# Memory products of block 2's second layer moved into block 1's norms, first layer's memory kept in DRAM, two modulations on VectorE

## The chip, the cores and the metric

The kernel runs on one core of a Trainium2 chip. The metric is the device time of one execution in microseconds, the median of the runs. PE is the matrix engine (TensorE), DVE VectorE, ACT ScalarE, POOL GpSimd; SP's queue issues the transfers.

## The reference

Two blocks work on a sequence of 256 tokens with 1024 channels in float32. Block 1 has two layers. In each, six modulation vectors are made from a condition vector, and each of two norms is scaled and shifted by a pair of them:

```python
mod = c_act @ w_ada[l] + b_ada[l]
sh1, sc1, g1, sh2, sc2, g2 = [t[:, None, :] for t in jnp.split(mod, N_ADA, axis=-1)]
h = rmsnorm(x, norm_mix_g[l]) * (1.0 + sc1) + sh1
z = h @ w_in[l]
...
x = x + g1 * (o @ w_out[l])
h = rmsnorm(x, norm_mlp_g[l]) * (1.0 + sc2) + sh2
x = x + g2 * (jnp.square(jax.nn.relu(h @ w_up[l])) @ w_down[l])
```

(o comes from four attention mixers on slices of z.) A last rmsnorm gives the input of block 2. Each of block 2's two layers has three branches: a state-space scan in two directions (32 heads), a differential attention of 8 heads, and a cross attention to a fixed memory of 256 tokens. The gated branches are summed, go through an output product, and end in a layer norm:

```python
mem_kv = jnp.einsum('bmd,de->bme', mem, w_mem_kv[layer]).reshape(
    Bsz, MEM_TOKENS, 2, CROSS_HEADS, CROSS_HEAD_DIM)
oc = _memory_cross_attention(cq.reshape(Bsz, S, CROSS_HEADS, CROSS_HEAD_DIM), mem_kv)
...
out = jnp.einsum('bsd,de->bse', merged, w_out[layer])

x = _layernorm(DEEPNORM_ALPHA * x.astype(jnp.float32) + out,
               ln_g[layer], ln_b[layer]).astype(x.dtype)
```

`mem_kv` holds the memory's keys and values. They depend on nothing that the blocks compute, so their products can stand anywhere before the layer that uses them.

## The kernel before

**Products.** Activations lie with channels on the partitions. Every product is split for accuracy: a weight tile `w` [128x1024] is cast to `wh` on ACT (L300) and the rest `wl` is taken on DVE (L302); the activations have a high and a low part too, and three products (h·wh, l·wh, h·wl, all at L328) are accumulated. A key piece of the memory is 48 products of 256 columns, a value half 48 products of 512 columns (`mem_gemm`, six pieces a layer: four for the keys, two for the values).

**Weights.** `stream` lists the weight tiles in the order of use, `next_w` takes the next one and at that time issues the transfers of the first eight entries of the list (L290, SP's queue) and splits the first four. There are eight buffers for `w` and four each for `wh` and `wl`.

**Order.** The program is written as one stream of instructions for all engines; a scheduler orders each engine's list at build time by readiness and priority. Fillers are closures in a queue: `fill` emits the next ones, `need` all up to a tag. Each engine then runs its list in order.

**Units.** Large activations live in eleven buffers of [128x2048] (`unit`). Whoever asks for a unit when all are taken waits in the schedule until the oldest user is done. In block 2 such units are, among others, `xh`, `xl` (the layer's input), `dq`, `dk`, `dv` (differential attention), `ysh`, `ysl` (the scan's output, two each), `mk` and `mv` (the memory).

**Norms.** `rms_wide` squares x on ACT, folds the squares on DVE, sums over partitions on PE (`st`), takes the rest on DVE (`rv`) and POOL (`rsy`, a power of -1/2, L394), and spreads it with PE (`bc`). Then DVE and ACT make `ah` and `al` (L590 to L592), slice by slice, and the next products start. In block 1 PE does a modulation (`ada`, 64 rows in the trace) meanwhile: the one for (layer 0, vector 5) in the norm before the first MLP, (1,2) and (1,3) before layer 1's mixers, (1,4) before the second MLP. In the first MLP POOL makes (1,0) and (1,1) with multiplications of its own (`sb`, L570 and L572), in the second (1,5). Before the final norm lies the second half of the first layer's memory values.

**Layer norm between block 2's layers.** The mean and the variance need two such rounds: st, mu, bc, subtraction (L1662), squares, folds, st, rv, rsy, bc. All six memory products of the second layer (`mem_gemm`, tile names mh and ml) are emitted there, and the scheduler spreads them over the rounds.

**Heads.** `diff` makes one head of the differential attention: scores (`ds`), softmax on DVE and ACT (`sm`, `E`), turning (`tw`), values (`do`); after four heads a norm on POOL scales their outputs (`rsy`, then eight times `dq`, L1603), and eight transposes (`dtp`, L1607) turn them. Fillers are emitted between the heads.

Of the kernel before, what the change touches and what calls it, by code (L numbers as in the profile page):

```python
# [216 lines left out]
AHEAD_W, AHEAD_S = 8, 4  # L217
# [8 lines left out]
class Emit:  # L226
# [100 lines left out]
    def mm(self, o, l, r, start, stop):  # L327
        self.nc.tensor.matmul(o, l, r, start=start, stop=stop)  # L328
# [37 lines left out]
    def tok_mm(self, ps, t, act, k, w, j, st, sp):  # L366

        wh, wl = (x[:, j * 512 : (j + 1) * 512] for x in w)
# [116 lines left out]
def block1(e, ctx, mem0):  # L485
# [3 lines left out]
    mhl, mk0, mv0 = mem0  # L489
# [16 lines left out]
    start = [[], a0[0:2], a0[2:4], a0[4:6], a0[6:8]]  # L506
    for k in range(MEM):
        e.stream(MEM_KEYS(0)[k], *start[k])
    for l in range(DEPTH):
        W = lambda i: ("w_in1", l, zorder[i])  # L510
        ea, am = ad_early(l), ad_mix(l)
        e.stream(*([] if l else [W(0)]), W(1), W(2), *ea[0:2], ("cmp_k1", l), W(3), *ea[2:3], ("cmp_v1", l), W(4), *ea[3:4], W(5))
        e.stream(W(6), *am[0:2], ("w_out1", l, 0), *am[2:3], W(7), ("w_out1", l, 1), *am[3:4], W(8), *am[4:])
        e.stream(("w_out1", l, 2), ("w_out1", l, 3), ("w_up", l, 0), *ad_norm(l))
# [6 lines left out]
        e.stream(("w_down", l, 15), *([("w_in1", l + 1, zorder[0])] if l + 1 < DEPTH else []), *ad_next(l))  # L521
    e.stream(*MEM_KEYS(0)[MEM:])
# [13 lines left out]
    boxes = {}  # L536
# [36 lines left out]

    def ada_rows(l, s):
# [8 lines left out]
    def norm_stats(src):  # L583
        return e.rms_wide(ap_, src, 1e-6)
# [23 lines left out]
    e.need("start4")  # L608

# [98 lines left out]
    def mixers(l, ah, al, oh, ol, ev_x):  # L708
# [258 lines left out]
        e.need("I")  # L967
        e.need("ad")
# [4 lines left out]
    for l in range(DEPTH):  # L973
# [4 lines left out]
        if l:  # L978
            bc0 = norm_stats(x)
            e.need("next")  # L980
# [12 lines left out]
        ada_add("norm", ad_norm(l))  # L993
        bc0 = norm_stats(x)
# [7 lines left out]
        def ev_up(g):  # L1002
            def ev(ps):
# [4 lines left out]
                last["act"] = nc.scalar.activation(uh, r, AF.Square)  # L1008
                nc.vector.tensor_tensor(r, r, ps, ALU.mult)
                last["dve"] = nc.vector.tensor_tensor(ul, r, uh.bitcast(F32), ALU.subtract)  # L1010
# [34 lines left out]
        def late_mem():  # L1045
            with tc.issue_after(last["dve"].ins), tc.issue_after(last["act"].ins):
                box.append(load_mem(e))

        parts, box, last = {}, [], {}
        steps = mlp_keys(l)  # L1050
        for g in range(17):
            if l + 1 == DEPTH and g == 1:
                e.add("mlp", late_mem)
# [7 lines left out]
            ada_add("mlp", steps.get(g, []))  # L1061
            for i, p in enumerate(ad_mlp(l)):
# [3 lines left out]
        ada_add("next", ad_next(l))  # L1066
# [14 lines left out]
    return xh, xl  # L1081
# [3 lines left out]
def block2(e, ctx, xh, xl, mk, mv, out):  # L1085
# [68 lines left out]
    for l in range(DEPTH):  # L1154
# [17 lines left out]
        if l + 1 < DEPTH:  # L1172
            e.stream(*MEM_KEYS(l + 1))
# [534 lines left out]
```

## Time and profile before

| | us |
|---|---|
| median of 3 runs (1836.12 to 1838.73) | 1838.46 |
| the profiled execution | 1837.75 |
| its span | 1835.9 |
| PE busy | 1785.1 (97% of the span) |
| DVE busy | 1332.7 (73%) |
| ACT busy | 1017.0 (55%) |
| POOL busy | 360.6 (20%) |

A busy PE is not a PE at its peak: products are pipelined, and the granted clock can be at either of two levels. The page gives the granted clock as a share of 2.4 GHz, so 0.50 is 1.2 GHz. Where PE has nothing to wait for, products of 256 columns follow each other every 0.12 us although each row shows 0.28. In the timelines, a row's bracket names the idle time of that engine before the row and what ended it; "x64" joins 64 like instructions in one row.

### The profile page before, as it was taken

The page shows a single profiled execution, that of the slowest core. Times are in us where ns is not written, and L with a number is a line of the kernel's source. Part 1 is how long each engine was busy: PE and PEld are TensorE (multiplying, and loading weights), DVE is VectorE, ACT ScalarE, POOL GpSimd, SP SyncE. Part 2 cuts the span into 40 slices and gives each one's busy share as a digit, 9 for nine tenths or more (in the row PEclk, how much of TensorE's full clock was granted, in tenths as well). Part 3 has the DMA queues.
Part 4 walks back from the last instruction along what each step waited for, and adds up shares of the span by engine and source line. Part 5 has one row for each costly group of instructions (what it writes and reads, how often), then busy time and mean ns, then how long its engine had stood idle before and what let it go on. Part 6 is the DMA issues. An engine that isn't in the chain of part 4 may idle for free.

```text
span 1835.9 us, 36208 instructions
## 1 busy us (share of the span) xinstructions
PE 1785.1 (97%) x14320; PEld 1671.4 (91%) x14320; DVE 1332.7 (73%) x2204; ACT 1017.0 (55%) x1882; POOL 360.6 (20%) x291
## 2 busy tenths in 40 slices
PE   7999899999998999999999999999999999999997
PEld 6778799987878999998999999999998999999996
DVE  3566775756768655798897997566788797997565
ACT  4444444444554444567777575454556777575452
POOL 0000282800007300002444202200001444202200
PEclk9999999999998999999999999999999999999999
DMA  8874876768347655553444644465554445644451
GB/s 330 305 233 159 316 259 199 254 201 294 128 143 280 225 181 184 170 170 122 159 162 152 195 159 145 167 206 174 196 175 138 150 154 158 194 162 162 151 183 57
DMA packets 98219, 346.82 MB, mean 189 GB/s; under 512 B 12288, under 2 KB 13440, under 8 KB 97792
## 3 DMA queue, kind: packets, MB, share of 16 engines
q1 hardware_dynamic: 98048, 344.50, 55.7%
q8 instruction: 112, 1.84, 0.4%
q14 instruction: 59, 0.48, 0.1%
HBM read 339.01 MB, written 1.05 MB: 185 GB/s over the span
## 4 chain that ended last, share of the span: by engine, by line
PE 91%; DVE 3%; ACT 3%; DMA 2%; issue 1%; POOL 0%; SPq 0%; POOLq 0%; DVEq 0%; ACTq 0%
PE g L328 68%; PE acc L328 10%; PE yps L328 2%; PE ada L328 1%; PE o L328 1%; DVE wl L302 1%; PE sc L328 1%; PE ds L328 1%; ACT wh L300 1%; PE do L328 1%; PE xs L328 1%; PE xo L328 1%; ACT sb L666 1%; DMA w<-w_up 1%; PE tp L691 1%
## 5 line engine op out<-in xcount | busy, mean ns | idle before, releaser
L302 DVE TENSOR_TENSOR wl<-w,wh 128x1024 fp32r<-128x1024 f32 x518 | 664.5, 1286 | 345.5 <-ACT wh L300 342.4
L300 ACT CAST wh<-w 128x1024 fp32r<-128x1024 f32 x518 | 540.7, 1047 | 504.6 <-PE g L328 339.5
L328 PE MATMUL g<-xh,wh 128*128 128x256 f32 x1664 | 477.7, 287 | 2.1 <-ACT dv L1291 1.9
L328 PE MATMUL g<-xl,wh 128*128 128x256 f32 x1664 | 472.1, 284 | 0.0
L328 PE MATMUL g<-xh,wl 128*128 128x256 f32 x1664 | 471.5, 283 | 0.0
L328 PEld LDWEIGHTS g<-xh,wh 128*128 128x128 f32 x1664 | 319.2, 192 | 14.5 <-issue 6.2
L328 PEld LDWEIGHTS g<-xl,wh 128*128 128x128 f32 x1664 | 319.5, 192 | 0.9 <-issue 0.7
L328 PEld LDWEIGHTS g<-xh,wl 128*128 128x128 f32 x1664 | 319.6, 192 | 0.0
L328 PE MATMUL g<-ah,wh 128*128 128x256 f32 x736 | 212.1, 290 | 6.8 <-ACT ah L591 6.7
L328 PE MATMUL g<-ah,wl 128*128 128x256 f32 x736 | 211.6, 288 | 1.2 <-DVE wl L302 1.2
L328 PE MATMUL g<-al,wh 128*128 128x256 f32 x736 | 211.5, 288 | 0.7 <-DVE al L592 0.5
L394 POOL TENSOR_TENSOR rsy<-rv,mhalf 128x2 f32<-128x2 f32 (+1 forms) x14 | 15.2, 1088 | 937.6 <-DVE rv L411 828.4
L328 PE MATMUL acc<-pt,wh 128*128 128x256 f32 x1024 | 182.9, 280 | 0.0
L1485 POOL PARTITION_BROADCAST E<-rows x64 | 95.2, 1547 | 387.9 <-PE tw L1192 185.4
L328 PEld LDWEIGHTS acc<-pt,wh 128*128 128x128 f32 x1024 | 156.8, 188 | 0.5 <-issue 0.4
L1484 ACT ACTIVATE E<-E,ltok 128x128 f32<-128x128 f32 x384 | 124.4, 394 | 59.2 <-POOL E L1485 55.5
L328 PEld LDWEIGHTS g<-ah,wh 128*128 128x128 f32 x736 | 143.0, 195 | 11.0 <-ACT ah L591 7.6
L328 PEld LDWEIGHTS g<-al,wh 128*128 128x128 f32 x736 | 143.5, 195 | 2.8 <-DVE al L592 2.0
L328 PEld LDWEIGHTS g<-ah,wl 128*128 128x128 f32 x736 | 143.4, 195 | 2.3 <-DVE wl L302 1.6
L328 PE MATMUL acc<-pt,wl 128*128 128x256 f32 x512 | 142.3, 279 | 0.0
L570 POOL TENSOR_SCALAR sb<-w,ca 128x1024 f32<-128x1024 f32 x24 | 90.0, 3750 | 61.9 <-PE ada L328 32.8
L328 PEld LDWEIGHTS acc<-pt,wl 128*128 128x128 f32 x512 | 96.2, 188 | 0.0
(384 smaller groups left out, 3386.3 us busy)
## 6 DMA issues: line engine op xcount, KB each, us to landing
w<-w_ada SPq DMA_DIRECT2D x96, 512.0 KB
w<-w_up SPq DMA_DIRECT2D x64, 512.0 KB
w<-w_down SPq DMA_DIRECT2D x64, 512.0 KB
w<-w_br SPq DMA_DIRECT2D x64, 512.0 KB
w<-w_gl SPq DMA_DIRECT2D x48, 512.0 KB
w<-w_in SPq DMA_DIRECT2D x36, 512.0 KB
w<-w_xs SPq DMA_DIRECT2D x32, 512.0 KB
w<-w_z SPq DMA_DIRECT2D x32, 512.0 KB
```

The lines of the kernel that those rows point to most:

```text
L300: nc.scalar.copy(wh, w)
L302: nc.vector.tensor_tensor(wl, w, wh.bitcast(F32), ALU.subtract)
L328: self.nc.tensor.matmul(o, l, r, start=start, stop=stop)
L394: self.nc.gpsimd.tensor_tensor(y, v, self.mhalf[:, 0:cols], ALU.pow)
L570: nc.gpsimd.tensor_scalar(dst, w, ca[:, 2 * n + i : 2 * n + i + 1], None, ALU.mult)
L666: nc.scalar.activation(self.src(i), self.src(i), AF.Exp, bias=nmx[:, i : i + 1], scale=scale, accum_out=den[:, i : i + 1])
L691: nc.tensor.transpose(tp[:, h * P : (h + 1) * P], src(h), e.ident)
L1484: ex = lambda o, s, r: nc.scalar.activation(o, o, AF.Exp, bias=bias[:, s, r : r + 1])
L1485: nc.gpsimd.partition_broadcast(E, state["rows"][32 * (h % 4) : 32 * (h % 4) + 1, :])
```

## The change

1. Four of the second layer's keys pieces and half of its values are computed in block 1's norms: key pieces 0 and 1 before the first MLP, 2 and 3 before layer 1's mixers, the first half of the values before the second MLP; the first layer's last half stays in the final norm. `rms_wide` gets three counts and places fillers before st, between st and bc, and behind bc, held to their place by `issue_after`. One half of the values is left in block 2's layer norm. The memory's activations are loaded at the end of both layers' mixers.
2. The units for the second layer's keys and values (`mem1`) are taken at the start and kept through block 2's first layer. The first layer's (1.5 MB) are written to DRAM at the start and read back in the second MLP (`reload`).
3. Modulations (0,5) and (1,2) are made on DVE in the first MLP (`ada_vec`, 16 operations of 128x1024, weights fetched into units of their own); PE only sums over partitions. (1,3) and (1,4) go into layer 1's mixers, as products.
4. At the start, the last half of modulation (0,1) stands before the last half of the first memory values' piece.
5. At the end, the last output product is split into token half 0 with 512 columns, then token half 1 twice with 256 columns, in that order by `issue_after`.
6. `next_w` looks over the whole list: it splits the next four entries that need it and fetches up to eight more.

```diff
     def next_w(self, *key):
-        for i, ent in enumerate(self.wq[:AHEAD_W]):
-            self._fetch(ent)
-            if i < AHEAD_S and ent[3] is None:
-                self._split(ent)
+        split = raw = 0
+        for ent in self.wq:
+            if not self._whole(ent) and split < NS:
+                split += 1
+                self._fetch(ent)
+                if ent[3] is None:
+                    self._split(ent)
+            elif raw < NW:
+                raw += 1
+                self._fetch(ent)
+                if self._whole(ent):
+                    ent[3] = ent[2]
+            else:
+                break
...
-    def rms_wide(self, pool, x, eps):
+    def rms_wide(self, pool, x, eps, before=0, between=0, behind=0):
+
         box = []
+        self.fill(before)
         with self.tc.high_priority(offset=NORM_FIRST):
             for j in range(4):
                 self.square(pool, box, flat(x[:, 2 * j : 2 * j + 2, :]))
-            return self.rstd(pool, self.fold_sum(box), D, eps)
+            st = self.fold_sum(box)
+        with self.tc.issue_after(self.last_mm.ins):
+            self.fill(between)
+        with self.tc.high_priority(offset=NORM_FIRST):
+            bc = self.rstd(pool, st, D, eps)
+        with self.tc.issue_after(self.last_mm.ins):
+            self.fill(behind)
+        return bc
...
-    ad_early = lambda l: ada(l, 2) if l == 0 else []
-    ad_mix = lambda l: ada(l, 3) + ada(l, 4) if l == 0 else []
-    ad_norm = lambda l: ada(l,5) if l == 0 else ada(l,4)
-    ad_mlp = lambda l: [(1,0),(1,1)] if l == 0 else [(1,5)]
-    ad_next = lambda l: ada(l+1,2)+ada(l+1,3)
+    ad_early = lambda l: ada(0, 2) if l == 0 else ada(1, 3)
+    ad_mix = lambda l: ada(0, 3) + ada(0, 4) if l == 0 else ada(1, 4)
+    ad_mlp = lambda l: [(1, 0), (1, 1)] if l == 0 else [(1, 5)]
+    ad_vec = lambda l: ada(0, 5) + ada(1, 2) if l == 0 else []
...
+    mem1 = MEM_KEYS(1)
+    filler = [mem1[0:2], mem1[4:5], mem1[2:4], MEM_KEYS(0)[MEM:]]
...
+    def reload():
+
+        back.extend((v3(e.unit("mk"), KC), v3(e.unit("mv"), 2)))
+        nc.sync.dma_start(back[0], mkd)
+        nc.sync.dma_start(back[1][:, :, 0:512], mvd)
...
+    def ada_fetch(l, s, n):
+        boxes["w", l, s, n] = e.unit("adaw")
+        nc.sync.dma_start(boxes["w", l, s, n], d["w_ada"][l, s, n])
+
+    def ada_vec(l, s, n):
...
+        for i in range(2):
+            c = ca[:, 2 * n + i : 2 * n + i + 1]
+            with tc.issue_after(last["ev"].ins):
+                if n == 0 and i == 0:
+                    nc.vector.tensor_scalar(rows, w[:, i, :], c, None, ALU.mult)
+                else:
+                    nc.vector.scalar_tensor_tensor(rows, w[:, i, :], c, rows, ALU.mult, ALU.add)
...
     e.need("start4")
+    e.need("start5")
+    dram = ctx.enter_context(tc.tile_pool(name="d1", bufs=1, space=bass.MemoryType.DRAM))
+    mkd, mvd = e.t(dram, [P, KC, S], "mkd"), e.t(dram, [P, 2, 512], "mvd")
+    nc.sync.dma_start(mkd, mk0)
+    nc.sync.dma_start(mvd, mv0[:, :, 0:512])
...
         if l:
-            bc0 = norm_stats(x)
+            bc0 = norm_stats(x, 2, 1, 1)
...
-        ada_add("norm", ad_norm(l))
-        bc0 = norm_stats(x)
+        mem_fill("norm", filler[l])
+        bc0 = norm_stats(x, 2, 1, 1)
...
-        ada_add("next", ad_next(l))
+        mem_fill("next", filler[DEPTH + l])
...
-    for k in range(MEM, 6):
-        mem_gemm(e, 0, k, box[0], mk0, mv0)
-    bc = norm_stats(x)
-    e.need("mem")
+    bc = norm_stats(x, 3, 1)
+    e.need("next")
...
-        for t in range(2):
-            ps = e.gbank("g")
-            for k in range(KC):
-                e.tok_mm(ps, t, hl, k, ws[k // 2], k % 2, k == 0, k == KC - 1)
-            ev(ps, 1, t)
-            norm(t)
+        for t, cols in ((0, (0, 512)), (1, (0, S)), (1, (S, 512))):
+            ps = e.gbank("g")[:, cols[0] : cols[1]]
+            with tc.issue_after(e.last_mm.ins):
+                for k in range(KC):
+                    e.tok_mm(ps, t, hl, k, ws[k // 2], k % 2, k == 0, k == KC - 1, cols)
+            ev(ps, 512 + cols[0], t)
+            if cols[1] == 512:
+                norm(t)
...
-        nmk, nmv = v3(e.unit("mk"), KC), v3(e.unit("mv"), 2)
+        nmk, nmv = mem1
         mhl = load_mem(e)
         e.need("out")
-        for i in range(6):
-            mem_gemm(e, l + 1, i, mhl, nmk, nmv)
+        mem_gemm(e, l + 1, 5, mhl, nmk, nmv)
...
-        mk, mv = v3(e.unit("mk"), KC), v3(e.unit("mv"), 2)
+        mk, mv, *mem1 = (v3(e.unit(n), k) for n, k in (("mk", KC), ("mv", 2)) * 2)
```

The order of PE's instructions, from the kernel before and from the changed one, at three places (with "..." where products of the same kind are left out).

The norm before the second MLP, on PE; `ada` is a modulation, `g<-wh,mh` a memory value product, `g<-ah,wh` the MLP's first product. Before:

```order
L328 MATMUL ada_6161<-w_6174,ca_11_101 32x256 x4
L328 MATMUL st_6151<-ones_72,fold_6142 128x1 x2
L328 MATMUL bc_6158<-pack_1_70,rsy_6156 128x128 x2
L328 MATMUL adat_6216<-pack_1_70,pt_1013_6214 128x4 x2
L328 MATMUL g_6258<-ah_6136,wh_6032 128x256
```

Changed:

```order
L337 MATMUL g_6437<-wh_6350,ml_6237 128x512
L337 MATMUL st_6475<-ones_72,fold_6466 128x1 x2
L337 MATMUL g_6430<-wh_6386,mh_6236 128x512
...
L337 MATMUL g_6437<-wh_6386,ml_6237 128x512
L337 MATMUL bc_6500<-pack_1_70,rsy_6498 128x128 x2
L337 MATMUL g_6430<-wh_6424,mh_6236 128x512
...
L337 MATMUL g_6437<-wh_6424,ml_6237 128x512
L337 MATMUL g_6561<-ah_6422,wh_6444 128x256
```

Ahead of st stand 24 memory products, between st and bc 12, behind bc 12. In the norms before the first MLP and before layer 1's mixers these are 48, 24 and 24 of 256 columns; in the final norm 36, 12 and 0 of 512.

The layer norm between block 2's layers, on PE; `dt` is the next layer's first product. Before:

```order
L328 MATMUL st_14910<-ones_72,fold_14778 128x1 x2
L328 MATMUL g_14995<-mh_14644,wh_14875 128x256
...
L328 MATMUL bc_14914<-pack_1_70,mu_14908 128x128 x2
L328 MATMUL g_14995<-mh_14644,wh_14918 128x256
...
L328 MATMUL st_15120<-ones_72,fold_14985 128x1 x2
L328 MATMUL g_15130<-mh_14644,wh_15058 128x256
...
L328 MATMUL bc_15127<-pack_1_70,rsy_15125 128x128 x2
L328 MATMUL g_15239<-wl_15090,mh_14644 128x512
...
L328 MATMUL dt_15382<-xh_15192,wh_15322 128x256
```

Changed:

```order
L337 MATMUL g_15220<-wh_15214,mh_14941 128x512
L337 MATMUL st_15207<-ones_72,fold_15075 128x1 x2
L337 MATMUL g_15220<-wl_15216,mh_14941 128x512
...
L337 MATMUL g_15227<-wh_15214,ml_14942 128x512
L337 MATMUL bc_15211<-pack_1_70,mu_15205 128x128 x2
L337 MATMUL st_15307<-ones_72,fold_15258 128x1 x2
L337 MATMUL bc_15314<-pack_1_70,rsy_15312 128x128 x2
L337 MATMUL dt_15355<-xh_15317,wh_15234 128x256
```

Before, 54 memory products lie ahead of st, then 21, 96, 28 and 89 in the four stretches up to dt; now 37 ahead of st, 11 up to the first bc, and none after it.

The heads of block 2's layer 0, on PE, from the scan's norm (st, bc) on; `g<-ysh,wh` and `g<-ysl,wh` are products on the scan's output. Before:

```order
L328 MATMUL st_12845<-ones_72,fold_12272 128x1 x2
L328 MATMUL g_13078<-ysh_12092,wh_12999 128x256
...
L328 MATMUL bc_12852<-pack_1_70,rsy_12850 128x128 x2
L1192 MATMUL tw_12862<-pack_1_70,E_12646 128x128 x4
L328 MATMUL g_13078<-ysh_12093,wl_13081 128x256
...
L328 MATMUL do_12868<-dv_9428,pt_12861 128x128 x4
L328 MATMUL g_13245<-xl_8431,wh_13136 128x256
...
L1607 MATMUL dtp_12888<-pack_1_70,dq_11382 128x128
L328 MATMUL g_13348<-ysh_12092,wl_13214 128x256
...
L1607 MATMUL dtp_12894<-pack_1_70,dq_11382 128x128
L328 MATMUL ds_12908<-dk_11781,dq_11382 128x256
```

Changed:

```order
L337 MATMUL g_13377<-ysh_12391,wh_13078 128x256
L337 MATMUL st_13144<-ones_72,fold_12571 128x1 x2
L337 MATMUL bc_13151<-pack_1_70,rsy_13149 128x128 x2
L1262 MATMUL tw_13161<-pack_1_70,E_12945 128x128 x4
L337 MATMUL do_13167<-dv_9727,pt_13160 128x128 x4
L1680 MATMUL dtp_13187<-pack_1_70,dq_11681 128x128 x4
L1680 MATMUL dtp_13193<-pack_1_70,dq_11681 128x128
L337 MATMUL ds_13207<-dk_12080,dq_11681 128x256
...
L1262 MATMUL tw_13243<-pack_1_70,E_13126 128x128 x4
L1680 MATMUL dtp_13193<-pack_1_70,dq_11681 128x128 x3
L337 MATMUL do_13249<-dv_9727,pt_13242 128x128 x4
```

It goes on with ds, tw, do, ds and half a tw without a product between. Then come the products on ysl, whose unit is the one that dk had, and the last two heads among products.

## Rows read from the trace of the kernel before

**Rows 1.** The page's part 4: the chain that ended last, share by engine.

```profile
PE 91%; DVE 3%; ACT 3%; DMA 2%; issue 1%; POOL 0%; SPq 0%; POOLq 0%; DVEq 0%; ACTq 0%
```

**Rows 2.** The list of PE's waits: releaser, us in total, times, longest.

```profile
PE bc L328 <- POOL rsy L394: 7.1, 4, 4.5
...
PE o L328 <- ACT pt L693: 2.1, 1, 2.1
...
PE tp L691 <- DVE sb L678: 1.8, 1, 1.8
```

**Rows 3.** Windows: PE, PEld, DVE, ACT, POOL busy, PE's clock, DMA share, GB/s.

```profile
213.70:220.50 6.80, 6.21 (x27) 5.92 (x28) 6.24 (x15) 3.13 (x8) 3.36 (x2) 0.50 1.03 418
216.00:398.00 182.00, 182.00 (x1515) 180.36 (x1515) 121.19 (x108) 86.08 (x102) 97.19 (x30) 0.99 0.70 234
880.00:1050.00 170.00, 169.36 (x1368) 157.32 (x1367) 143.83 (x212) 122.54 (x270) 71.94 (x84) 1.00 0.51 162
1101.00:1166.00 65.00, 65.00 (x538) 62.86 (x536) 43.38 (x78) 35.55 (x83) 19.25 (x19) 1.00 0.44 147
```

**Rows 4.** Timeline of PE at block 1's norms: start, us, engine, line, operation, wait.

```profile
204.72 3.66 PE L328 MATMUL ada<-w,ca 128*32 128x256 f32 x64
...
210.02 0.71 PE L328 MATMUL bc<-pack,rsy 128*128 128x128 f32 x4 [1.10 <-POOL rsy L394]
...
213.76 0.79 PE L328 MATMUL g<-ah,wh 128*128 128x256 f32 x2 [2.64 <-ACT ah L591]
...
403.17 3.65 PE L328 MATMUL ada<-w,ca 128*32 128x256 f32 x62
...
421.86 0.50 PE L328 MATMUL adat<-pack,pt 128*128 128x4 f32 x4
...
545.31 3.66 PE L328 MATMUL ada<-w,ca 128*32 128x256 f32 x64
...
557.38 0.79 PE L328 MATMUL g<-ah,wh 128*128 128x256 f32 x2 [1.52 <-ACT ah L591]
...
757.53 0.71 PE L328 MATMUL bc<-pack,rsy 128*128 128x128 f32 x4 [1.05 <-POOL rsy L394]
```

**Rows 5.** Timeline, PE and DVE, layer norm of block 2's layer 0.

```profile
1279.70 0.60 PE L328 MATMUL bc<-pack,mu 128*128 128x128 f32 x4
...
1280.34 2.48 DVE L1662 TENSOR_TENSOR r<-r,bc 128x512 f32<-128x512 f32 x4 [1.75 <-PE bc L328]
...
1288.56 0.42 DVE L435 TENSOR_TENSOR fold<-fold 128x256 f32<-128x256 f32 x1
...
1316.88 0.28 PE L328 MATMUL dt<-xh,wh 128*128 128x256 f32 x1
```

**Rows 6.** Timeline of PE and DVE at the end of the program.

```profile
1825.18 0.39 PE L328 MATMUL g<-wl,gh 128*128 128x512 f32 x1
1825.41 0.39 PE L328 MATMUL g<-wh,gl 128*128 128x512 f32 x1
...
1829.85 0.15 DVE L1219 TENSOR_SCALAR rv<-mv 128x1 f32<-128x1 f32 x1
```

**Rows 7.** Timeline, PE, POOL, DVE, heads of block 2's layer 0.

```profile
1115.01 1.05 PE L328 MATMUL do<-dv,pt 128*128 128x128 f32 x8
...
1119.03 7.45 POOL L1603 TENSOR_SCALAR dq<-dq,rsy 128x128 f32<-128x128 f32 x8
...
1125.39 1.13 PE L328 MATMUL ds<-dk,dq 64*128 64x256 f32 x6
...
1142.58 1.29 DVE L1179 TENSOR_REDUCE sm<-ds 128x2 f32<-128x512 f32 x2 [0.85 <-PE ds L328]
...
1147.01 0.88 DVE L1581 SCALAR_TENSOR_TENSOR E<-E,sd,E 128x256 f32<-128x256 f32 x2
```

**Rows 8.** Timeline of POOL and DVE in the first MLP.

```profile
238.13 2.40 POOL L572 TENSOR_TENSOR sb<-sb,sb 128x1024 f32<-128x1024 f32 x1
...
238.74 4.01 DVE L302 TENSOR_TENSOR wl<-w,wh 128x1024 fp32r<-128x1024 f32 x2 [1.35 <-ACT wh L300]
```

More of the change, by code (lines that the diff above doesn't have):

```diff
@@ L488, in block1 @@
     cp, zp, ap_ = pool("c1"), pool("z1"), pool("a1")
-    mhl, mk0, mv0 = mem0
+    mhl, mk0, mv0, mk1, mv1 = mem0
     cT = e.p0["cT"]
@@ L505, in block1 @@
     a0 = ada(0, 0) + ada(0, 1)
-    start = [[], a0[0:2], a0[2:4], a0[4:6], a0[6:8]]
+    start = [[], a0[0:2], a0[2:4], a0[4:6], []]
+    mem1 = MEM_KEYS(1)
+    filler = [mem1[0:2], mem1[4:5], mem1[2:4], MEM_KEYS(0)[MEM:]]
     for k in range(MEM):
         e.stream(MEM_KEYS(0)[k], *start[k])
+    half = e.wq[-2:]
+    del e.wq[-2:]
+    e.stream(*a0[6:8])
+    e.wq.extend(half)
     for l in range(DEPTH):
@@ L534, in block1, with mem_fill @@
     mods = [e.t(cp, [P, 48], f"mod{l}") for l in range(DEPTH)]
-    boxes = {}
+    boxes, last, hl = {}, {}, []
+    def mem_fill(tag, steps):
+        for key in steps:
+            i = MEM_KEYS(key[1]).index(key)
+            mem_gemm(e, key[1], i, hl[-1], mk1 if key[1] else None, mv1 if key[1] else back[1], tag)
+    back = []
+    def reload():
+        back.extend((v3(e.unit("mk"), KC), v3(e.unit("mv"), 2)))
+        nc.sync.dma_start(back[0], mkd)
+        nc.sync.dma_start(back[1][:, :, 0:512], mvd)
     def ada_step(l, s, n):
@@ L572, in ada_pool @@
                 nc.gpsimd.tensor_tensor(rows, rows, dst, ALU.add)
+    def ada_fetch(l, s, n):
+        boxes["w", l, s, n] = e.unit("adaw")
+        nc.sync.dma_start(boxes["w", l, s, n], d["w_ada"][l, s, n])
+    def ada_vec(l, s, n):
+        if n == 0:
+            if "rows" not in boxes:
+                boxes["rows"] = v3(e.unit("rows"), 2)
+            boxes[l, s] = boxes["rows"][:, 0 if l == 0 else 1, :]
+        rows, w = boxes[l, s], v3(boxes.pop(("w", l, s, n)), 2)
+        for i in range(2):
[5 more added lines that the diff above has]
+                    nc.vector.scalar_tensor_tensor(rows, w[:, i, :], c, rows, ALU.mult, ALU.add)
+        if n == 3:
+            e.q.insert(min(6, len(e.q)), ("mlp", lambda: ada_rows(l, s)))
     def ada_rows(l, s):
@@ L597, in block1 @@
         ada_add(f"start{g}", start[g])
+    half = e.q[-2:]
+    del e.q[-2:]
+    ada_add("start4", a0[6:8])
+    e.q.extend(("start5", fn) for _, fn in half)
     b_ada = e.p0["b_ada"]
@@ L1043, in down_last @@
                     part(c, (m, m + 1))
[L1045 to L1049, printed above, removed]
+        vec = ad_vec(l)
+        at = lambda j: 3 + 3 * j // 2
+        parts = {}
         steps = mlp_keys(l)
@@ L1052, in block1 @@
             if l + 1 == DEPTH and g == 1:
-                e.add("mlp", late_mem)
+                e.add("mlp", reload)
+            for j, key in enumerate(vec):
+                if at(j) == g + 2:
+                    e.add("mlp", lambda key=key: ada_fetch(*key[1:]))
             if g < 16:
@@ L1061, in block1 @@
             ada_add("mlp", steps.get(g, []))
+            for j, key in enumerate(vec):
+                if at(j) == g:
+                    e.add("mlp", lambda key=key: ada_vec(*key[1:]))
             for i, p in enumerate(ad_mlp(l)):
@@ L1080, in block1, with block2 @@
                 e.split(xh[:, k - 1, :], xl[:, k - 1, :], x[:, k - 1, :])
-    return xh, xl
-def block2(e, ctx, xh, xl, mk, mv, out):
+    return xh, xl, *back
+def block2(e, ctx, xh, xl, mk, mv, mem1, out):
     nc, tc, d = e.nc, e.tc, e.d
@@ L1207, in finish, with ev @@
                 nc.scalar.activation(r[:, t, q * 512 : (q + 1) * 512], ps, AF.Copy, scale=ALPHA)
-        stats = e.t(tp_, [P, 2, 2, 6], "stats")
-        def ev(ps, g, t):
-            rg = r[:, t, g * 512 : (g + 1) * 512]
+        stats = e.t(tp_, [P, 2, 4, 6], "stats")
+        def ev(ps, c0, t):
+            rg = r[:, t, c0 : c0 + ps.shape[1]]
             nc.vector.tensor_tensor(rg, ps, rg, ALU.add)
-            nc.vector.bn_stats(out=stats[:, t, g, :], in_=rg)
+            for i in range(0, ps.shape[1], S):
+                nc.vector.bn_stats(out=stats[:, t, (c0 + i) // S, :], in_=rg[:, i : i + S])
         def norm(t):
```

36 lines of the change are left out of this document (17 added, 19 removed).

## The prediction

> **What bounds the kernel now.** I read the chain of waits first: it lies on TensorE (PE) for 91% of the span [rows 1]. So time is won or lost only where PE waits, works at the lower clock, or has work put on or taken off it. The list of PE's waits [rows 2] names the places: the broadcast bc of a norm behind GpSimd's (POOL's) power rsy, four times with 4.5 us the longest, and two attention waits of about 2 us in the layer-1 mixers. The windows [rows 3] show the rest of the program full: in block 2's layer 0 PE is busy 169.36 of 170 us during the scan and 65.00 of 65 during the attention heads. They also show what a wait leaves behind: for 6.8 us after the wait in the first MLP norm the granted clock is 0.50, the 1.2 GHz level. So I look at each place where the order of PE's instructions changes, and at what is late there.
>
> **The change part by part**, against the profiled execution (1837.75 us). A 256-column product is issued every 0.12 us, a 512-column one every 0.23 [rows 6]; a key piece of memory (48 products) is 5.8 us of PE, a half of the values 10.9.
>
> *Norm before the first MLP.* Before: from the modulation at 204.72 to the first product on ah at 213.76 [rows 4], 9.0 us, of which 3.66 are the modulation, and then 3.4 us lost at half clock [rows 3]. After: 48 products, st, 24, bc, 24, so 11.5 us of memory work and 0.8 of st and bc. From bc to ah takes 3.7 (210.02 to 213.76) against 24 products of 2.9 and bc itself: 0.4 idle, plus about 1.4 of pace behind ah and al at full clock. 14.4 against 12.4: **+2.0** with 11.5 us of work placed.
> *Norm before layer 1's mixers.* From 403.17 to the turned modulation at 421.86 plus 0.5 [rows 4] are 19.1 us with 48 products on ah in it (5.8), so 13.3 for the norm and two modulations. After, like the one above: about 14.9, **+1.6**.
> *Norm before the second MLP.* 545.31 to 557.38, and some 3.0 at half clock as above, 15.1. After: 24 wide products, st, 12, bc, 12, 11.7 with st and bc; 0.7 and 1.4 lost: **-1.3**.
> *Final norm.* The same half of the values lies there before and after; now 12 of its products stand between st and bc and 1.05 of wait [rows 4] goes, with some of the half clock behind: **-1.8**.
> *Layer norm at the end of block 2's layer 0.* Before, 288 products fill it: 4 x 5.8 + 2 x 10.9 + 1.7 of st and bc, 46.6 us, no wait. After, 48 wide ones are left, all of them ahead of bc(mu). From bc(mu) on nothing covers the chain. Its length before, from bc at 1279.70 through four subtractions (1280.34, 2.48) to the last fold at 1288.56 plus 0.42, holds other VectorE work and buffer waits; alone I take 6.5 us, then st, rv, rsy and bc (2.0) and 1.8 to dt. So 8.5 + 0.4 + 2.5 + 0.4 of products ahead, 10.3 of chain with next to no PE work, and some 3 us of ramp at half clock: 25.1 against 46.6: **-21.5** (-24 to -18).
> *Modulations.* Two of the four go to VectorE; PE keeps their sums over partitions, 16 short matmuls, at the spacing of the 64 that take 3.66, plus turning: **+1.2**. The other two, 7.3 us of PE, move into the layer-1 mixers, where the two waits of 2.1 and 1.8 [rows 2] can take some: 2.3 of it, so **+5.0** (+3 to +8). On VectorE: 16 operations of 128x1024; a 128x512 with two SBUF inputs costs 0.62 (2.48 for four, [rows 5]), so 1.25 each, 20 us beside 121.19 of 182 [rows 3]. PE is full there, the queue keeps four split tiles ahead: nothing. If each waited behind a POOL operation as the one in [rows 8], 2.0 each, 153 of 182, still nothing.
> *Start.* The last half of the modulation is put ahead of 24 products, whose 2.9 us now cover the turn to ah; against it stands the writing of 1.5 MB to DRAM on the same queue, 3.6 us at the 418 GB/s of [rows 3] if all of it delays weights. I take it as mostly hidden: **-2.5** (-2.9 to +0.7).
> *End.* The second token half ends one bank after the first: its rv, at 1829.85, comes 4.1 us after the last product at 1825.41 plus 0.39 [rows 6]; with the first half already through VectorE I expect 1.5. **-2.5** (-3.5 to -1).
> Reloading 1.5 MB in the second MLP and one more load of the memory: 0, the weights' queue has slack there.
>
> Together **-19.8**.
>
> **What speaks against it: the held units.** mk1 and mv1 now keep two of the eleven units through block 2's layer 0. The order shows the consequence. ysl gets its unit only when dk is free, after the last head's scores. Products on ys that stood between heads 3 to 7 (some 290 matmuls, 35 us) move behind them, and PE's row there is st, bc, tw, do, five dtp, ds, tw, three dtp, do, ds, tw, do, ds, half a tw. PE issues in order, so each wait of the heads is now its own. From do at 1115.01 to the next ds at 1125.39 are 10.4 us [rows 7]: squares, rsy, then POOL's eight scalings, 7.45 in all and five of them ahead of the fifth dtp. PE's own work in it is 1.05 and five short transposes, so about 8 us idle. Twice after that the softmax of one head is in the way: from its maximum at 1142.58 to the end of the last combination at 1147.01 plus 0.88 are 5.3 us, against 2.5 of PE work (tw, do, ds): 5.5 for both. With 1.0 for bc: 14.5 idle. Two such waits, each with some us at half clock behind it as in [rows 3], 4.5. **+19** (from 8, the dtp wait alone at full clock, to 25).
> *The scan.* Its units come late too: of its sixteen output groups eight are done early, then none for 38 us of PE work, then eight at about 6.2 us each where they came every 9.1. ScalarE (ACT) was busy 122.54 of 170 [rows 3], 6.6 per group: 0.4 for each of the later ones, less what is made ahead: **+2** (0 to +7).
>
> Sum: -19.8 + 19 + 2 = **+1.2**, 1838.95 by the profiled execution. The median of the runs is 0.7 above that, so **1839.7**. A measurement of this kernel can tell about 0.2% (3.7 us) from no change.
>
> **A rule weighed.** In [rows 8] a VectorE pair that starts inside a POOL operation takes 4.01 us instead of 2.5; it ends 2.2 us after POOL's does, about the time of the two. The Trainium skill, page "SBUF — State Buffer", section "Who interferes with whom", states that a VectorE instruction with two SBUF inputs contends with a GpSimd instruction that reads SBUF, and that whoever issues first holds the shared pair while the other fully blocks. By that rule taken as exclusive for all of them, VectorE's 121.19 + 20 and POOL's 97.19 would not fit into 182 us side by side, and the MLP would grow by up to 56. The trace agrees for this one pair, but the same sum is 218 before the change with PE busy 182.00 of 182, so it cannot hold for all.
>
> **The rivals.**
> *The heads' gap is half as long.* If POOL's scalings run faster once fewer VectorE operations lie beside them, and the clock does not fall, the gap is 9 and the scan 1: 1837.75 - 19.8 + 10 + 0.7 = **1828.7**. For it: the dtp in the trace before were spaced by products, so the chain may be shorter than 10.4. Against: the first scaling cannot start before rsy, whoever is idle. 0.29.
> *Slower: the units cost their full price.* Place: heads 3 to 7 and the second half of the scan. Price: 25 + 7, so 1837.75 - 19.8 + 32 + 0.7 = **1850.7**. It decides from 23.5 us on (19.8 + 3.7); at 19.8 it eats the whole gain. For it: all waits in that row are on an engine that issues in order, and the granted clock fell after shorter ones. 0.24.
> *VectorE and POOL exclude each other in the first MLP.* A mechanism of this kernel: 16 operations more, each held for one POOL operation (97.19 over 30 is 3.2 us, [rows 3]); wl comes late, PE waits. 16 x 3.2 is 52, less the 41 us that VectorE has free in the window after its 20: 11 us on top of the forecast, **1850.7**. Against: PE was full with 97 us of POOL there. 0.05.
>
> **How the numbers follow.** Forecast 0.42 (own range 1834 to 1846, of which 0.04 lies under and 0.12 over the 0.2%). Faster: 0.29 + 0.04 = 0.33. Slower: 0.24 + 0.05 + 0.12 = 0.41. Within: 0.26. The range goes from the faster rival to the slower: 1828 to 1851, leaving out about 0.2.
>
> **What would show it.** The layer norm from the last out product to dt should take 23 to 27 us, with 8 to 11 idle between bc(mu) and the second bc. In block 2's layer 0, dtp should wait 6 to 9 us on POOL's dq and tw 2 to 3 on E, with the clock at 0.5 behind. The bc waits in the norms should be under 0.5. In the first MLP PE should stay full and wl be under 2 us in the mean. I am wrong if the heads show no wait, if the norms still wait (weights late at DMA), or if the mixers of layer 1 lose more than the modulations' 7.3.

## The result

| | median, us | runs |
|---|---|---|
| before | 1837.29 | 4 (1835.90 to 1838.73) |
| changed | 1866.24 | 4 (1864.49 to 1868.12) |

The changed kernel is slower by 29 us: a ratio of 1.0158 (95% interval 1.0144 to 1.0171). The forecast was 1839.7 with a range of 1828 to 1851, so the time is 15 us beyond the range's end.

The head of the changed kernel's page (busy time, share of the span, instructions):

```profile
span 1866.3 us, 36044 instructions
...
PE 1804.5 (97%) x14232; PEld 1680.7 (90%) x14232; DVE 1358.3 (73%) x2227; ACT 1017.1 (54%) x1884; POOL 359.2 (19%) x291
```

PE is busy 19 us longer than before although two modulations (7.3 us) were taken off it but for their sums, and its share is still 97%. A PE that issues at half clock counts as busy, so the share says nothing here. The list of PE's waits (releaser, us in total, times, longest) answers to [rows 2]:

```profile
PE st L337 <- DVE fold L444: 14.5, 6, 6.4
PE g L337 <- ACT wh L299: 11.7, 3, 10.9
...
PE g L337 <- DVE al L650: 4.0, 2, 2.8
PE dtp L1680 <- POOL dq L1676: 3.6, 1, 3.6
PE bc L337 <- POOL rsy L403: 2.1, 2, 1.1
PE tw L1262 <- DVE E L1654: 1.9, 1, 1.9
```

The attention waits of the layer-1 mixers are gone and the waits of bc have fallen from 7.1 to 2.1 us, as meant. In their place st waits for the last fold (14.5 us, six times), g for al, and dtp for POOL's dq. I cut both traces at the same instructions: the first product on ah, the last product of an output, the last acc, the first dt and so on. Each row of the table is the time from the cut ahead, in us, and the second column holds the forecast's terms added to the first. (The sums of both of VectorE's modulations, 1.2 us, stand in the first MLP, where the trace has them.) Each column is one profiled execution.

| stage | before | forecast | changed | held units freed (mem1_dram) | POOL moved (pool_first) | both (dram_pool) |
|---|---|---|---|---|---|---|
| to the first product on ah | 62.3 | 59.8 | 64.4 | 63.9 | 64.4 | 63.8 |
| layer-0 mixers | 142.2 | 142.2 | 147.6 | 143.7 | 143.8 | 142.8 |
| first MLP with its norm | 198.4 | 201.6 | 205.9 | 206.0 | 203.3 | 203.3 |
| layer-1 norm and mixers | 142.1 | 148.7 | 150.1 | 152.5 | 150.1 | 154.0 |
| second MLP with its norm | 200.3 | 199.0 | 207.3 | 207.7 | 200.0 | 200.0 |
| final norm | 14.0 | 12.2 | 13.6 | 13.6 | 13.6 | 13.6 |
| block 2, layer 0, to its layer norm | 510.9 | 531.9 | 536.5 | 512.9 | 542.2 | 511.1 |
| layer norm | 46.6 | 25.1 | 22.8 | 22.8 | 22.8 | 22.8 |
| layer 1 to the last product | 508.9 | 508.9 | 510.6 | 510.9 | 512.6 | 510.7 |
| from there to the end of the span | 10.1 | 7.6 | 7.5 | 7.6 | 7.5 | 7.6 |

The layer norm, the end and the hole in block 2's layer 0 came about as forecast. What the forecast missed lies in block 1: the two MLPs with their norms (4.3 and 8.3 us), the start (4.6) and the first mixers (5.4).

**Block 2, layer 0.** The windows of the changed kernel (columns as in [rows 3]): the scan, the heads, and in the heads the stretch at half clock.

```profile
880.00:1050.00 170.00, 167.93 (x1279) 153.66 (x1277) 144.69 (x210) 127.69 (x280) 70.91 (x82) 1.00 0.46 153
1130.00:1170.00 40.00, 27.01 (x148) 21.48 (x147) 21.13 (x56) 15.67 (x51) 7.08 (x10) 0.70 0.12 40
1136.10:1160.00 23.90, 15.79 (x59) 11.37 (x60) 7.45 (x19) 5.69 (x21) 7.08 (x10) 0.50 0.07 23
```

Where 65 of 65 us were busy in [rows 3], 27.01 of 40 are now, and for 23.9 us the clock is 0.50. The timeline of that stretch (start, us, engine, line, operation, wait) answers to [rows 7]:

```profile
1137.61 1.01 PE L337 MATMUL st<-ones,fold 128*128 128x1 f32 x4 [3.83 <-DVE fold L444]
1139.71 0.58 PE L337 MATMUL bc<-pack,rsy 128*128 128x128 f32 x1 [1.08 <-POOL rsy L403]
...
1142.46 2.08 PE L337 MATMUL do<-dv,pt 128*128 128x128 f32 x8 [0.68 <-ACT pt L1263]
...
1147.51 4.69 POOL L1676 TENSOR_SCALAR dq<-dq,rsy 128x128 f32<-128x128 f32 x8
...
1148.18 2.81 PE L1680 MATMUL dtp<-pack,dq 128*128 128x128 f32 x5 [3.64 <-POOL dq L1676]
1150.92 1.65 PE L337 MATMUL ds<-dk,dq 64*128 64x256 f32 x6
...
1165.13 0.41 PE L1262 MATMUL tw<-pack,E 128*128 128x128 f32 x2 [1.89 <-DVE E L1654]
```

The row of PE is the one that the order announced: st, bc, tw, do, then dtp held for 3.64 us by POOL, then ds. POOL needs 4.69 us for its eight scalings where it took 7.45 before, so this wait is shorter than the 8 us that I took. But st also waits 3.83 us, for the fold of the scan's norm, and from then on each operation takes twice as long: do 2.08 against 1.05, ds 2.08 against about 1.1. The idle time from st's wait to tw's at 1165.13 adds up to 12.5 us (14.5 forecast). The heads, from the first ds to the layer norm's first memory product, lost 22.6 us. The rest of that, some 10, is mostly the low clock (4.5 forecast): PE's busy time over the heads grew from 231.22 to 240.54 us for the same 1914 instructions.

**The norm before the second MLP**, in the changed kernel, on POOL, DVE and PE:

```profile
573.46 6.37 POOL L607 TENSOR_SCALAR sb<-w,ca 128x1024 f32<-128x1024 f32 x2 [117.66 <-DMA w<-w_ada]
579.80 0.72 POOL L403 TENSOR_TENSOR rsy<-rv,mhalf 128x2 f32<-128x2 f32 x1
...
587.95 3.22 POOL L607 TENSOR_SCALAR sb<-w,ca 128x1024 f32<-128x1024 f32 x1 [5.07 <-DMA w<-w_ada]
...
573.59 2.05 DVE L301 TENSOR_TENSOR wl<-w,wh 128x1024 fp32r<-128x1024 f32 x1 [0.54 <-ACT wh L299]
575.57 0.41 DVE L444 TENSOR_TENSOR fold<-fold 128x256 f32<-128x256 f32 x1
...
577.04 0.15 DVE L420 TENSOR_SCALAR rv<-st 128x2 f32<-128x2 f32 x1
...
591.68 4.20 DVE L301 TENSOR_TENSOR wl<-w,wh 128x1024 fp32r<-128x1024 f32 x2 [0.52 <-ACT wh L299]
...
576.04 0.79 PE L337 MATMUL st<-ones,fold 128*128 128x1 f32 x4 [2.21 <-DVE fold L444]
...
580.94 0.61 PE L337 MATMUL bc<-pack,rsy 128*128 128x128 f32 x4
...
584.95 0.50 PE L337 MATMUL g<-ah,wh 128*128 128x256 f32 x2 [0.65 <-ACT ah L649]
...
597.11 0.58 PE L337 MATMUL g<-al,wh 128*128 128x256 f32 x1 [2.76 <-DVE al L650]
```

This answers to 545.31 and 557.38 in [rows 4]. Two of POOL's modulation products (sb) start at 573.46, inside the norm, and take 6.37 us. The norm's power rsy stands behind them: rv is written by 577.19, rsy starts at 579.80. While sb runs, a split on VectorE takes 2.05 us (1.2 alone), and behind the norm two of them take 4.20, with al queued behind them: 2.76 us of wait at 597.11. Ahead of that, st waited 2.21 us for the fold, which has splits of the memory's weights ahead of it on VectorE. In the kernel before, POOL's row has the other order, and the first sb of this MLP started after bc (554.00):

```profile
552.32 1.62 POOL L394 TENSOR_TENSOR rsy<-rv,mhalf 128x2 f32<-128x2 f32 x1 [115.28 <-DVE rv L411]
556.20 5.67 POOL L570 TENSOR_SCALAR sb<-w,ca 128x1024 f32<-128x1024 f32 x2 [2.26 <-DMA w<-w_ada]
```

In the norm before the first MLP the changed kernel has sb ahead of rsy too:

```profile
215.98 5.92 POOL L607 TENSOR_SCALAR sb<-w,ca 128x1024 f32<-128x1024 f32 x2 [126.94 <-DMA w<-w_ada]
221.87 0.72 POOL L403 TENSOR_TENSOR rsy<-rv,mhalf 128x2 f32<-128x2 f32 x1
```

There rsy starts only 0.55 us after rv is written (221.32); rv itself is late, behind a split that took 2.05 us beside sb.

**The start.** The last weight tile of the memory's values is cast at 56.32, as it lands; the products that were to cover the turn wait for its second half:

```profile
56.32 1.04 ACT L299 CAST wh<-w 128x1024 fp32r<-128x1024 f32 x1 [0.83 <-DMA w<-w_mv]
...
57.71 0.79 PE L337 MATMUL g<-wl,mh 128*128 128x512 f32 x1 [1.43 <-DVE wl L301]
```

### The profile page after: what moved, and what is told of

The parts are those of the page before. It is cut to its first block, busy times and chain, and to the rows that moved or that the text cites. A ratio compares the mean times of both kernels' runs of the same rounds, so it can differ in the third digit from the quotient of the medians.

```text
span 1866.3 us, 36044 instructions
## 1 busy us (share of the span) xinstructions
PE 1804.5 (97%) x14232; PEld 1680.7 (90%) x14232; DVE 1358.3 (73%) x2227; ACT 1017.1 (54%) x1884; POOL 359.2 (19%) x291
## 4 chain that ended last, share of the span: by engine, by line
PE 63%; DVE 2%; ACT 1%; issue 1%; POOL 0%; POOLq 0%; DVEq 0%; ACTq 0%
PE g L337 51%; PE acc L337 5%; PE yps L337 2%; PE ds L337 1%; PE xo L337 1%; PE xs L337 1%; PE do L337 1%; DVE wl L301 1%; PE tw L1262 1%; PE dt L337 0%; PE gp L337 0%; PE xtp L1545 0%; ACT E L1557 0%; ACT E L1253 0%; ACT wh L299 0%
## 5 line engine op out<-in xcount | busy, mean ns | idle before, releaser
L337 PEld LDWEIGHTS g<-al,wh 128*128 128x128 f32 x736 | 142.1, 193 | 5.6 <-DVE al L650 4.9
```

What stands on the lines that cost most here:

```text
L337: self.last_mm = self.nc.tensor.matmul(o, l, r, start=start, stop=stop)
```

## The experiments

**The held units.** The second layer's keys and first value half go to DRAM too and come back at the layer norm (mem1_dram):

```diff
+        nc.sync.dma_start(mkd1, mk1)
+        nc.sync.dma_start(mvd1, mv1[:, :, 0:512])
...
-        nmk, nmv = mem1
+        nmk, nmv = v3(e.unit("mk"), KC), v3(e.unit("mv"), 2)
+        nc.sync.dma_start(nmk, mem1[0])
+        nc.sync.dma_start(nmv[:, :, 0:512], mem1[1])
```

> The changed kernel, but the second layer's keys and first half of values are written to DRAM early in the second MLP and read back at block 2's layer norm, so that their two units are free in block 2's layer 0. Theory U (the held units made the heads and the scan lose): PE's list has its products between the heads again; from the first dt to the first memory product of the layer norm it should take 511 us as before instead of 536.5, the dtp wait of 3.6 us and the half-clock stretch of 24 us from 1136 on should be gone, span about 1866 - 25 = 1841. Rival (the heads lose because ScalarE and VectorE are late there anyway, or the 24 us at half clock have another cause): within 5 us of 1866.

Measured: span 1841.5, 24.8 us less. Block 2's layer 0 takes 512.9 us, the scan 155.1 as before (160.4 in the changed kernel), and the heads are full again at full clock (window of mem1_dram):

```profile
1100.00:1166.00 66.00, 66.00 (x542) 63.49 (x541) 54.27 (x105) 44.04 (x103) 9.84 (x10) 1.00 0.48 156
```

So the two held units cost 23.6 of the 25.6 us that this stage had lost. In the 2.0 us left lies one wait of 2.9 us (do for pt on VectorE), which dram_pool below does not have; it has 0.2 left. The layer-1 mixers, whose PE list the scheduler ordered otherwise here, took 2.4 us more than in the changed kernel, and the first mixers 3.9 less.

**POOL's modulations.** In the changed kernel they are streamed from the second step of an MLP on. First, all of them two steps later (pool_later):

```diff
-    mlp_keys = lambda l: {1 + 6 * i + n: [("w_ada", *p, n)] for i, p in enumerate(ad_mlp(l)) for n in range(4)}
+    mlp_keys = lambda l: {3 + 6 * i + n: [("w_ada", *p, n)] for i, p in enumerate(ad_mlp(l)) for n in range(4)}
...
-                if g == 6 * i + 8:
+                if g == 6 * i + 10:
```

> The changed kernel, with GpSimd's modulations (the sb operations) streamed and emitted two steps later in both MLPs. In the changed kernel two sb of 5.9 and 6.4 us started inside the norms, ahead of rsy on GpSimd's list. Theory P (that is what made the two MLP norms long: rsy behind sb, and VectorE's wl and al held by them): rsy follows rv within 0.3 us, and from the last out product to the first product on ah it falls from 15.6 and 16.9 us by 1 and 3 us, with 1 to 3 us more off the stretch behind it; span -4 to -10. Rival S (it is the splits: the casts wh on ScalarE and wl on VectorE for the memory pieces stand between the squares and folds, so that st waits for the fold): st still waits 1.4 and 2.2 us for the fold, both norms stay within 1.5 us of 15.6 and 16.9, span within 3 us.

Measured: span 1865.9, no gain. The norms fell as theory P has it, from 15.6 to 13.3 us and from 16.9 to 13.7, and the MLPs with them by 4.4 and 7.3 us in all. But the norm before layer 1's mixers went from 13.3 to 20.5 (timelines of DVE and PE in pool_later):

```profile
413.05 0.17 DVE L596 TENSOR_TENSOR mod<-adat,pack 128x8 f32<-128x8 f32 x1 [1.42 <-PE adat L337]
...
417.52 1.48 DVE L438 TENSOR_TENSOR fold<-fold,pt 128x512 f32<-128x512 f32 x2
419.04 0.43 DVE L444 TENSOR_TENSOR fold<-fold 128x256 f32<-128x256 f32 x1
...
412.51 0.50 PE L337 MATMUL adat<-pack,pt 128*128 128x4 f32 x4
...
419.52 1.01 PE L337 MATMUL st<-ones,fold 128*128 128x1 f32 x4 [4.14 <-DVE fold L444]
```

The second modulation's sum now ends inside that norm: mod is ready at 413.05, the folds come late behind it, and st waits 4.14 us. Of the 11.7 us won in the two MLPs the third norm took back 7.2. That the span shows no gain at all is due to block 2, which this edit does not touch: its layer 0 took 6.0 and its layer 1 3.5 us more than in the profiled execution of the changed kernel, the start and the first mixers together 5.4 less. So only the first modulation of each MLP is moved (pool_first):

```diff
+    mlp_keys = lambda l: {(3 if i == 0 else 7) + n: [("w_ada", *p, n)] for i, p in enumerate(ad_mlp(l)) for n in range(4)}
...
+                if g == (9 if i == 0 else 14):
```

> The changed kernel, with only the first of GpSimd's modulations in each MLP moved two steps later (the second stays, so that it ends in time for the norm before layer 1's mixers, where the run with both moved lost 7 us). Theory P (rsy stood behind sb on GpSimd's list, and VectorE behind GpSimd): the first MLP with its norm, from the last out product to the last acc product, falls from 205.9 to about 202, the second from 207.3 to about 200, the norm before layer 1's mixers stays at 13.3; up to the first dt 10 to 13 us less than the changed kernel's 789.0. Rival: the 7 us come back elsewhere in block 1, so that the first dt stays above 784.

Measured: first dt at 775.2 instead of 789.0, the two MLPs 203.3 and 200.0, the third norm 13.3. Of the 13.8 us up to the first dt, 9.9 lie in the two MLPs; 3.8 lie in the first mixers, ahead of everything that the edit changes, and are luck. The span is 1860.2, 6 us less and not 14, since block 2's layer 0, with its units still held, takes 5.7 us more in this execution. The norm before the second MLP, on POOL and PE:

```profile
570.00 0.70 POOL L403 TENSOR_TENSOR rsy<-rv,mhalf 128x2 f32<-128x2 f32 x1 [120.63 <-DVE rv L420]
594.41 5.68 POOL L607 TENSOR_SCALAR sb<-w,ca 128x1024 f32<-128x1024 f32 x2 [23.71 <-DMA w<-w_ada]
...
568.77 0.60 PE L337 MATMUL st<-ones,fold 128*128 128x1 f32 x4 [1.38 <-DVE fold L444]
...
572.09 0.61 PE L337 MATMUL bc<-pack,rsy 128*128 128x128 f32 x4
```

rsy follows rv at once, the first sb comes 24 us later, bc has no wait. The 1.38 us for the fold stay: on VectorE a split of 1.23 us stands right ahead of that fold (at 567.16). That part is rival S, and it is the small one.

**The weights' window** of before in the changed kernel (old_window):

```diff
-        split = raw = 0
...
+        for i, ent in enumerate(self.wq[:AHEAD_W]):
+            self._fetch(ent)
+            if i < AHEAD_S and ent[3] is None:
+                self._split(ent)
```

> The changed kernel with the weights' window of before (the first eight entries of the list fetched, the first four split). Theory W (the deeper window brings the modulations' weights early and crowds out the others: the start, the half-clock stretches at 105 and 142 us in the first mixers, and GpSimd's early start follow from it): first product on ah at 62 to 63 instead of 64.4, the first mixers 142 to 144 us instead of 147.6, span -5 to -10. Rival (the window is not the cause; GpSimd's list has sb ahead of rsy in either case): first ah at 64, mixers at 147, span within 3 us of 1866.

Measured: span 1865.8; first product on ah 64.3, the MLP norms 15.6 and 16.7, as in the changed kernel. The window is the cause of neither, so theory W falls for the start and the norms. For the first mixers it does not: they took 141.4 us here and 140.8 in the repaired kernel with the old window (below), against 142.8 to 147.6 with the deeper one and the same start. That is some 2 us, which the times alone cannot tell.

**The start's order** of before in the changed kernel (start_before):

```diff
-    start = [[], a0[0:2], a0[2:4], a0[4:6], []]
+    start = [[], a0[0:2], a0[2:4], a0[4:6], a0[6:8]]
```

> The changed kernel with the order of the start as before: the last half of modulation (0,1) behind the last half of the first memory values. The writes of 1.5 MB to DRAM stay. Theory O (the new order itself costs: the last 24 products now wait for the last weight tile and its split, where before only short modulation products stood behind the last transfer): first product on ah at about 62.3 as before, instead of 64.4. Rival D (the writes to DRAM or the window delay the weights): it stays at 64 or goes up to 67.

Measured: first product on ah 62.1, as before the change, but the mixers' output ends no earlier than in the other runs (207.0; 205.7 to 212.0), since 6.8 us at half clock follow. Span 1869.5. The new order shifts a wait of 2.5 us and does not remove it.

**Both repairs** (dram_pool):

> Both repairs together: the second layer's memory through DRAM, and GpSimd's first modulation of each MLP two steps later. If the two causes are independent, the gains add: 1866 - 25 - 11 = 1830, about 8 us under the kernel before. If the norms' loss was hidden behind something else, it stays near 1841.

Measured: 1831.47 us, median of 10 runs, ratio to before 0.9972 (0.9960 to 0.9983); the profiled span is 1829.7. The two causes add, and without them the kernel is no longer slower than the one before. They are not all that the forecast missed: without the held units its terms add up to -19.8 us, and the kernel is 5.4 us faster. Against these terms the start lacks 4.0 us, the first MLP 1.7, the final norm 1.4, the second MLP 1.0 and block 2's layer 1 1.8; the layer-1 norm and mixers lack 5.3. That last stage took 152.4 to 155.1 us in the six kernels with this repair and 150.1 to 150.3 in four without it (pool_later, the fifth, lost 7.2 in its norm). The scheduler ordered PE's list in these mixers otherwise once the repair was in, and no run separates what in the new order costs the time.

**The layer norm's products spread** over its chain, on top of that (dram_pool_ln):

```diff
+        e.fill(1)
+        st = e.fold_sum(lst)
+        with tc.issue_after(e.last_mm.ins):
+            e.fill(1)
...
+        with tc.issue_after(e.last_mm.ins):
+            e.fill(2)
```

> As dram_pool, with the one memory product that is left in block 2's layer norm spread over its chain: 12 products ahead of the first st, 12 up to the first bc, 24 behind it, where 37, 11 and 0 stood. Theory L (the wait of 6.4 us for the last fold and the 10 us at half clock behind it are uncovered chain): from the first memory product to dt 16 to 18 us instead of 22.8, so 5 to 7 us less than dram_pool. Rival (the products' splits stand in the way of the folds, or the chain itself is that long): over 21 us.

Measured: the layer norm takes 20.2 us instead of 22.8, the kernel 1831.24 us, ratio 0.9967 (0.9953 to 0.9982), not told from dram_pool. PE in the layer norm of the changed kernel, and then of dram_pool_ln:

```profile
1333.86 0.50 PE L337 MATMUL st<-ones,fold 128*128 128x1 f32 x4
...
1336.84 0.61 PE L337 MATMUL bc<-pack,mu 128*128 128x128 f32 x4
1343.81 1.01 PE L337 MATMUL st<-ones,fold 128*128 128x1 f32 x4 [6.36 <-DVE fold L444]
1345.88 1.22 PE L337 MATMUL bc<-pack,rsy 128*128 128x128 f32 x4 [1.06 <-POOL rsy L403]
1348.22 0.58 PE L337 MATMUL dt<-xh,wh 128*128 128x256 f32 x1 [1.12 <-ACT xh L1744]
```

```profile
1293.41 0.61 PE L337 MATMUL st<-ones,fold 128*128 128x1 f32 x4 [0.96 <-DVE fold L444]
...
1296.71 0.61 PE L337 MATMUL bc<-pack,mu 128*128 128x128 f32 x4
...
1305.63 0.69 PE L337 MATMUL st<-ones,fold 128*128 128x1 f32 x4 [2.84 <-DVE fold L444]
...
1309.71 0.58 PE L337 MATMUL dt<-xh,wh 128*128 128x256 f32 x1 [1.11 <-ACT xh L1751]
```

The wait for the last fold falls from 6.36 to 2.84 us, but a new one of 0.96 stands ahead and the whole is only 2.6 us shorter. From the first bc to the second st it takes 8.9 us, where the changed kernel takes 7.0. VectorE's row shows why, with three splits between the subtraction and the last fold, where dram_pool has one (at 1303.07):

```profile
1299.75 1.22 DVE L301 TENSOR_TENSOR wl<-w,wh 128x1024 fp32r<-128x1024 f32 x1
...
1301.49 1.21 DVE L301 TENSOR_TENSOR wl<-w,wh 128x1024 fp32r<-128x1024 f32 x1
...
1304.02 1.22 DVE L301 TENSOR_TENSOR wl<-w,wh 128x1024 fp32r<-128x1024 f32 x1
```

So the outcome lies between both: theory L held for the wait, and the rival's splits in the way of the folds took part of the gain. How long the chain is without them no run shows.

**The end alone**, in the kernel before (before_end): the diff's last output product in three parts, with statistics by 256 columns.

> The kernel before with the change at the end of the program alone (last output product in three parts). From the last product's start to the end of the span 10.1 us before, 7.5 in the changed kernel: I expect 2.5 us less than the kernel before, within what can be told at its edge. Rival (the gain at the end is eaten by the extra products' part): no difference in span.

Measured: 1835.34 against 1836.84, ratio 0.9994 (0.9982 to 1.0007), no difference that the times can tell. In its trace the last product ends at 1825.88, within 0.1 us of the kernel before, and the span ends 2.7 us earlier. The last product and rv in the changed kernel, to be read with [rows 6]:

```profile
1858.54 0.28 PE L337 MATMUL g<-wh,gl 128*128 128x256 f32 x1
...
1860.07 0.15 DVE L1290 TENSOR_SCALAR rv<-mv 128x1 f32<-128x1 f32 x1
```

**Start and window again**, with both repairs in:

> dram_pool with the order of the start as before the change. In the run with only this undone the first product on ah came at 62.1 instead of 64.4, but a half-clock stretch of 6.8 us lay behind it instead of 3.4 ahead, and the first mixers ended no earlier. If the new start order is worth what I forecast for it (2.5 us), this is 2 to 3 us slower than dram_pool; if it is worth nothing, the end of the first mixers' output stays at 206 to 208 and the time within 1.5 us of dram_pool's 1831.5.

> dram_pool with the weights' window of before. If the deeper window is worth something in the layer-1 mixers, where two modulations' weights are among the split ones, this is slower by 2 us or more, with waits of the kind g behind wl or ada behind w_ada; if it is worth nothing, the time is within 1.5 us of dram_pool's 1831.5, as the window alone made no difference to the changed kernel.

> dram_pool with the start and the window of before and the layer norm's products spread. If the parts are independent: between 1828 and 1832; what would count against that is a time over 1834.

Measured, against 1838.61 for the kernel before on that chip: the old start 1834.02, ratio 0.9979 (0.9967 to 0.9991); the old window 1829.18, ratio **0.9947** (0.9930 to 0.9965); old start, old window and spread products 1829.69, ratio 0.9958 (0.9943 to 0.9973). The old start is 2.5 us above dram_pool's 1831.47 and the old window 2.3 below, both more than the 1.5 us that was to mean nothing; but the kernel before differed by 1.8 us between the two sets of runs, and the ratios' intervals overlap with dram_pool's. So neither the start nor the window is shown to matter. The version with the old window beats both kernels, by about 9 us the one before.

## Why the prediction was wrong

Term by term, against the stages above:

- **Layer norm** (-21.5): -23.8, with 7.4 us of idle time where I had named 8 to 11. **End** (-2.5): -2.6. **Final norm** (-1.8): -0.4, since the wait that remained was dt's, now 1.5 us. **Modulations and the norm in layer 1** (+1.6 and +5.0): +8.0. **VectorE's modulations** at nothing: the first MLP behind its norm takes 190.3 us against 189.2, the splits there have a mean of 1.38 us (1.46 before), and PE waits 2.0 us in all. The sums of the two modulations take some 2.5 us of PE, where 1.2 was forecast. Beside POOL's operations the splits are slow where they meet: 2.05 us for one, 4.20 for two in the norm's rows. The Trainium skill, page "SBUF — State Buffer", section "Who interferes with whom", has VectorE with two SBUF inputs and GpSimd's reads exclude each other. The trace agrees in part: the split at 573.59 was slowed (2.05 against 1.2), but it ended at 575.65, inside the sb that had begun before it and ended at 576.31. Taken as exclusive throughout, the MLP would have grown by up to 56 us, and it grew by 1.
- **The held units** (+19 and +2): +22.6 in the heads and +5.3 in the scan (the stretch ahead of the scan took 2.4 us less), shown by mem1_dram. The mechanism was the forecast one; its size was under by 7, nearer to the slower rival's 32 than to my 21. The half clock was taken at 4.5 us where it was about 10, and the scan at 2. The idle time came out at 12.5 for 14.5 by luck: st's wait of 3.83 us for the scan's fold was not in my list, and dtp's, forecast at about 8, was 3.64. The faster rival was right that POOL's scalings would run faster, and wrong that the clock would not fall.
- **The two MLP norms** (+2.0 and -1.3, with 1.2 of sums in the first MLP): +7.5 and +7.0. This is the step that failed. (By its own terms the first norm's 14.4 us add up to 14.1, so +1.7.) I worked out how long the memory products cover the chain and took the chain itself from the kernel before. POOL's list had changed too: two sb had moved from behind rsy to ahead of it in both norms. Why the build put them there is only argued (four weight tiles of the memory stand where eight of the modulation stood, so the next ones come in sooner); the window is not it, as old_window has the same order. The order of POOL's instructions showed it; I had read PE's and not POOL's. "The bc waits in the norms should be under 0.5" was the sign I named, and bc did not wait, because 24 narrow or 12 wide products lay between: the delay showed as late products, half clock behind st, and al. Moving the first modulation gives 203.3 and 200.0 us, +4.9 and -0.3. What remains of the first is 4.1 in the norm, most of it the placed products as forecast (st's wait for the fold is 0.6 us there), and 0.8 behind it, where the sums cost more than the half clock of before gave back.
- **The start** (-2.5): +2.1 at the first product, about 0 to +2 at the end of the first mixers. I took the products as ready; their last weights land at 56.3 and are then split.
- **The first mixers** (0): +5.4 in the profiled execution. Six runs with the same PE list there took 142.8 to 147.6 us, with half-clock stretches at 105 in some and at 142 in one (behind a wait of 1.13 us for a modulation's weights), so most of it is this execution's and not the change's. That is as far as the runs tell; what lets the clock fall at 105, where PE does not wait, stays open.

The two norms' 12.6 us are the largest miss, but the 15 us beyond the range's end take more than one: the start and the first mixers add 4.6 and 5.4, the held units 4.6. The range's upper end was set by one loss at a time. The rival in block 1, POOL against VectorE, had part of the mechanism, but placed it in the first MLP and not in the norms, and was not added to the held units.

## What to carry to other kernels

When a change moves fillers into a chain, read the list of every engine that the chain passes, not only of the engine that the filler runs on: here two operations that moved ahead of a power of 0.7 us on GpSimd cost about 10 us in two norms and the MLPs behind them. A buffer that is held longer costs where buffers are scarce, which can be two stages away; parking it in DRAM gave back 23.6 us in that stage for 1.5 MB written and read. And a gain that takes away waits is lost again where a longer wait lets the clock fall: count the work behind a wait at the lower clock too.

## What the runs showed of the hardware

POOL's eight scalings of 128x128 took 4.69 us with VectorE idle beside them (0.60 each), 7.45 with VectorE at work (1.33 to 1.64 for the three that met a split). PE did 15.79 us of rows in 23.9 us at 0.50, and kept that clock over a row of waits of 0.7 to 3.6 us, behind one of 3.8. With the products back between the heads (mem1_dram) PE had no wait there and the whole stretch was at 1.00.
